# Two fp32r passes for the attention scores, gate columns on the output-gate slab, and the first block loaded ahead

## The chip, the cores and the metric

The kernel runs on one core of a Trainium2 chip. The metric is the device time of one execution in microseconds; a run is compared by the median of its timed executions, and one further execution is profiled.

## The reference

A decoder trunk of two layers over 512 tokens of width 1024, in fp32. Each layer computes, cut to what the change touches:

```python
h = rmsnorm(x, norm_mix[i])
proj = h @ w_in[i]            # 3088 columns: q 512, k 512, v 512, conv 3 x 256, gla q 128, k 128, v 256, gate 256, low-rank gate 16
q, k = rope(q), rope(k)       # 4 heads x 2 maps x 64
for each block of 128 queries: # differential attention
    s = (q @ k.T) / 8, causal
    a = softmax(s[:, map 0]) - lam * softmax(s[:, map 1])
    o_da = rmsnorm(a @ v) * gain * (1 - lam_init)
o_sc = B * conv3(C * h_in)
log_a = log_sigmoid(g_lr @ gla_w_gate2 + gla_b_gate) / 16
o_g = rmsnorm(gla(g_q, g_k, g_v, log_a)) * silu(g_r)
x = x + concat(o_da, o_sc, o_g) @ w_out[i]
x = x + peer(rmsnorm(x, norm_ffn[i]))      # 16384 single-neuron experts
```

## The kernel before

Tokens stand in four blocks of 128 (TB = 4), visited in ORDER = (3, 0, 1, 2) by the first normalisation. Each layer is `mixer` (about the first 286 us) and `peer` (the rest). Projections are done in split precision: an operand is a high part, rounded to fp32r, and a low part, the remainder, and `mm3` forms high x high, high x low and low x high in three single-pass matmuls. The split costs a ScalarE cast and a VectorE subtraction (`split`, L79).

`setup` loads all four blocks of x (L93), then the identity; `norm_T` (L176) loads the gain row, computes each block's statistics, normalises into a scratch tile and transposes it into hh and hl. Scratch is the space of va and kT.

`slab` (L234) brings a slab of w_in, 8 x 128 rows by n columns, in four quarters: a load into `wraw` (three buffers), then the split into wh and wl (two buffers each, so one slab can be prepared while another is used). `across` (L247) uses the slab as stationary operand, 24 matmuls of 512 columns per 128 slab columns; `down` (L256) uses hh and hl as stationary, 24 matmuls of n columns per token block. The slabs come in the order gla v (2560), low-rank gate (3072, 16 columns padded to 128), gla q and k (2304), output gate (2816), q and k (0 to 768, each rotated and transposed by `rope_T`), v (1024, 1280), and three for the convolution (2048, 1792, 1536).

`gla` (L483) is a generator: a first piece from the gate matmul to the cumulated decay b, then six levels that fill masked score tiles, the state recurrence, and the outputs. `fill` (L305) advances it between the slabs, against due times written by hand.

`diff_attention` (L425) multiplies, for each head and map, a query tile qz whose other map's 64 rows are zero with kT, both in fp32; then the causal mask (bf16) is added in PSUM, and VectorE and ScalarE do the softmax. Blocks 0 and 1 are computed between the convolution's slabs, blocks 2 and 3 after them, while w_out is loaded in eight rows of 128 x 1024 through two `woraw` buffers and split (L357). `out_proj` (L371) has 48 matmuls of 512 columns a token block and starts with the last normalisation's transposes.

The framework keeps each engine's instructions in an order that a planner works out at build time by priority (program order) and its own estimate of when things are ready; loads on SP's queue are in such an order too. Only instructions marked so stay in program order, in `peer`. A tile that is laid over the space of older tiles waits for their last readers.

Of the kernel before, what the change touches and what calls it, by code (L numbers as in the profile page):

```python
# [19 lines left out]
P = 128  # L20
T = 512
# [42 lines left out]
class K:  # L64
# [18 lines left out]
    def setup(self):  # L83
# [9 lines left out]
        for tb in ORDER:  # L93
            nc.sync.dma_start(self.x[:, tb], self.ins["x"][tb * P:(tb + 1) * P, :])
# [3 lines left out]
        nc.sync.dma_start(self.ident, self.ins["c_ident"])  # L98

# [101 lines left out]
    def mixer(self, L):  # L201
# [3 lines left out]
        with ExitStack() as mc:  # L205
            mp = mc.enter_context(tc.tile_pool(name="mix", bufs=1, reuse_waits="tile"))
            lamv = mp.tile([P, 4, 64], F32, name="lamv")
# [3 lines left out]
            kT = mp.tile([P, 4, T], F32, name="kT")  # L211
# [3 lines left out]
            norm = self.norm_T(ins["norm_mix"][L:L + 1, :], hh, hl, rows(va) + rows(kT), order=ORDER)  # L215
            with ExitStack() as wc:
# [7 lines left out]
                z = qp.tile([P, 2, T + 2], F32, name="z", bufs=1)  # L224
                nc.vector.memset(z[:, :, 0:2], 0.0)
# [8 lines left out]
                def slab(c0, n):  # L234
# [3 lines left out]
                    for kh in range(0, KD, 2):  # L238
                        raw = wp.tile([P, 2, w], F32, tag="wraw", name="wraw", bufs=3)
# [28 lines left out]
                wh, wl = slab(2560, 256)  # L268
                for i, tb in enumerate(ORDER):
# [11 lines left out]
                lt = mp.tile([P, 64], F32, name="lt")  # L281
# [10 lines left out]
                for j, ps in across(3072, 16):  # L292
                    nc.scalar.copy(lr, ps[0:16])
# [8 lines left out]
                side = self.gla(L, gq, gk, gv, sg, lr, mgh, mgl, gp)  # L302
# [7 lines left out]
                fill(10)  # L310
                for i in range(4):
                    for tbs, ps in down(256 * i):
                        self.rope_T(ps, (qT, kT)[i // 2], i % 2, tbs, qp)
                    fill(10 + 10.5 * (i + 1))
                for i in range(2):
                    for tbs, ps in down(1024 + 256 * i):
                        nc.scalar.copy(va[:, tbs, 256 * i:256 * i + 256], ps)
                    fill(52 + 10.5 * (i + 1))
# [4 lines left out]
                qz = [ap.tile([P, 4, 2, P], F32, name=f"qz{i}", bufs=1) for i in range(2)]  # L323
                for t in qz:
                    nc.gpsimd.memset(t, 0.0)
                heads = []

                def attend(tb):
                    heads.append(self.diff_attention(tb, qT, kT, va, qz[tb % 2], lam, ap))
# [20 lines left out]
            with tc.tile_pool(name="wout", bufs=1, reuse_waits="tile") as op_:  # L350
                wr = [op_.tile([P, D], F32, tag="woraw", name="woraw", bufs=2) for _ in range(2)]
                mh = op_.tile([P, 4, T], F32R, name="mh")
                ml = op_.tile([P, 4, T], F32R, name="ml")
# [3 lines left out]
                for k in korder:  # L357
                    raw = wr.pop(0) if wr else op_.tile([P, D], F32, tag="woraw", name="woraw", bufs=2)
# [3 lines left out]
                def chunk(k, s):  # L362
                    if k < 4:
                        return mh[:, k, s], ml[:, k, s]
                    a, b = (mch, mcl) if k < 6 else (mgh, mgl)
                    return a[:, k % 2, s], b[:, k % 2, s]
# [4 lines left out]
                def out_proj(tb):  # L371
                    for nh in range(2):
                        ps = self.psC.tile([P, T], F32, tag="c", name="pso")
                        n = slice(nh * 512, nh * 512 + 512)
                        for k in korder:
                            self.mm3(ps, *chunk(k, slice(tb * P, tb * P + P)), wh[:, k, n], wl[:, k, n],
# [5 lines left out]
                for tb in range(TB):  # L382
                    if tb > 1:
                        attend(tb)
                    t = slice(tb * P, tb * P + P)
                    self.head_out(heads[tb], dgain, mh[:, 0:4, t], ml[:, 0:4, t])
# [691 lines left out]
```

## Time and profile before

| | |
|---|---|
| median of three runs | 3034.66 us (3029.43 to 3035.7) |
| profiled execution, own time | 3031.94 us |
| its span in the profile | 3030.2 us |
| TensorE busy | 2964.8 us (98%) |
| VectorE busy | 2440.4 us (81%) |
| ScalarE busy | 1270.5 us (42%) |
| GpSimd busy | 690.1 us (23%) |
| mean DMA rate | 250 GB/s |
| mean granted TensorE clock | 0.997 |

Busy time is the union of an engine's instructions. Matmuls are pipelined, so that one that is 0.40 us long can be followed by the next after 0.23 us; what a matmul costs is read from the starts in the order of time. The span is the profiled execution from its first to its last instruction; its own time has the 1.7 us around it as well.

### The profile page before, as it was taken

Reading aid. Unit: us, or ns where it says so; the run is one execution under the profiler, and the core shown is the slowest. Engines: PE = TensorE matmul, PEld = TensorE weight load, DVE = VectorE, ACT = ScalarE, POOL = GpSimd, SP = SyncE. Lnnn points to the kernel's source line nnn. Section 1 sums busy time; section 2 is a strip of 40 time slices with the busy share of each in tenths; the row PEclk is TensorE's granted clock in tenths of the full one; section 3 lists DMA queues with packets and bytes.
Section 4 is the critical chain, followed back from the end, with each engine's and each line's share of the span. In section 5 each row is a group of like instructions: output and inputs, shape, how many; then the busy total and the mean of one; then the engine's idle time right before and its main releaser. Section 6 shows DMA issues by size and latency. Waiting matters only on the chain.

```text
span 3030.2 us, 45706 instructions
## 1 busy us (share of the span) xinstructions
PE 2964.8 (98%) x16742; PEld 2650.7 (87%) x16742; DVE 2440.4 (81%) x5057; ACT 1270.5 (42%) x1874; POOL 690.1 (23%) x553
## 2 busy tenths in 40 slices
PE   7999999999999999999999999999999999999998
PEld 7977899999999999788889788999999999988886
DVE  5766999977788787877766769999868887878777
ACT  5343346556333333333353533565563333323333
POOL 0000000222444444211100000002224544452120
PEclk9999999999999999999999999999999999999999
DMA  4212248899999998999722222579999999989996
GB/s 122 67 57 78 96 142 256 279 300 340 341 332 333 325 337 299 349 337 329 290 78 67 73 72 91 173 245 296 313 352 328 336 335 333 332 299 343 341 347 225
DMA packets 335697, 756.64 MB, mean 250 GB/s; under 512 B 31568, under 2 KB 192240, under 8 KB 331376
## 3 DMA queue, kind: packets, MB, share of 16 engines
q1 hardware_dynamic: 141936, 406.60, 37.8%
q0 software_dynamic: 73728, 268.47, 24.7%
q10 hardware_dynamic: 119808, 78.66, 8.3%
q8 instruction: 131, 2.15, 0.3%
q14 instruction: 94, 0.77, 0.1%
HBM read 672.89 MB, written 80.74 MB: 249 GB/s over the span
## 4 chain that ended last, share of the span: by engine, by line
PE 76%; DVE 11%; issue 4%; DMA 3%; ACT 3%; POOL 1%; ACTq 1%; SPq 0%; DVEq 0%; POOLq 0%
PE pv L76 10%; PE pv L77 10%; PE pv L75 10%; PE psh L75 8%; PE psh L77 8%; PE psh L76 8%; PE psp L77 2%; PE psp L76 2%; PE psp L75 2%; PE psq L75 2%; PE psq L76 2%; PE psq L77 2%; DVE ul L651 1%; DMA row<-in_v_rows,idx 1%; POOL row L737 1%
## 5 line engine op out<-in xcount | busy, mean ns | idle before, releaser
L75 PE MATMUL psh<-ahi,uh 128*128 128x384 f32 x2048 | 692.2, 338 | 6.6 <-ACT ht L665 6.6
L77 PE MATMUL psh<-ahi,ul 128*128 128x384 f32 x2048 | 687.5, 336 | 0.0
L76 PE MATMUL psh<-alo,uh 128*128 128x384 f32 x2048 | 686.3, 335 | 0.0
L737 POOL DMA_INDIRECT row<-in_u_rows,idx x256 | 364.5, 1424 | 1342.6 <-DVE si L905 689.0
L76 PE MATMUL pv<-vl,wh 128*128 128x512 f32 x1536 | 601.1, 392 | 6.9 <-DVE vl L828 6.9
L77 PE MATMUL pv<-vh,wl 128*128 128x512 f32 x1536 | 601.2, 392 | 0.0
L75 PE MATMUL pv<-vh,wh 128*128 128x512 f32 x1536 | 597.6, 390 | 0.0
L651 DVE TENSOR_TENSOR ul<-uraw,uh 128x1024 fp32r<-128x1024 f32 x288 | 350.9, 1221 | 210.8 <-ACT uh L650 200.5
L737 POOL DMA_INDIRECT row<-in_v_rows,idx x256 | 307.6, 1202 | 623.6 <-DVE yacc L754 589.9
L650 ACT CAST uh<-uraw 128x1024 fp32r<-128x1024 f32 x288 | 302.3, 1050 | 330.8 <-PE psh L76 99.5
L828 DVE TENSOR_TENSOR vl<-vraw,vh 128x1024 fp32r<-128x1024 f32 x256 | 313.1, 1223 | 128.1 <-ACT vh L833 118.3
L75 PEld LDWEIGHTS psh<-ahi,uh 128*128 128x128 f32 x2048 | 385.1, 188 | 14.1 <-ACT ht L665 9.7
L76 PEld LDWEIGHTS psh<-alo,uh 128*128 128x128 f32 x2048 | 385.1, 188 | 4.1
L77 PEld LDWEIGHTS psh<-ahi,ul 128*128 128x128 f32 x2048 | 385.0, 188 | 0.0
L76 PEld LDWEIGHTS pv<-vl,wh 128*128 128x128 f32 x1536 | 289.0, 188 | 66.8 <-DVE vl L828 8.7
L665 ACT ACTIVATE ht<-psh 128x384 f32<-128x384 f32 x256 | 125.2, 489 | 519.2 <-PE psh L77 512.6
L77 PEld LDWEIGHTS pv<-vh,wl 128*128 128x128 f32 x1536 | 289.0, 188 | 61.6 <-DVE wl L828 1.2
L754 DVE SCALAR_TENSOR_TENSOR yacc<-row,wk,yacc 128x1024 f32<-128x1024 f32 x254 | 325.1, 1280 | 18.3 <-DMA row<-in_v_rows,idx 16.8
L75 PEld LDWEIGHTS pv<-vh,wh 128*128 128x128 f32 x1536 | 289.0, 188 | 57.5
L842 ACT CAST wh<-ht 128x384 fp32r<-128x384 f32 x256 | 131.2, 512 | 492.9 <-DVE ht L840 482.0
L745 DVE SCALAR_TENSOR_TENSOR gscr<-row,xg 128x1024 f32<-128x1024 f32 x256 | 312.4, 1220 | 27.7 <-DMA row<-in_u_rows,idx 25.9
L833 ACT CAST vh<-vraw 128x1024 fp32r<-128x1024 f32 x256 | 268.5, 1049 | 7.5 <-DMA vraw<-in_v_rows 7.1
(289 smaller groups left out, 4396.3 us busy)
## 6 DMA issues: line engine op xcount, KB each, us to landing
uraw<-in_peer_u SPq DMA_DIRECT2D x256, 512.0 KB, 5.4
vraw<-in_v_rows SPq DMA_DIRECT2D x256, 512.0 KB, 6.0
G<-stg ACTq DMA_DIRECT2D x48, 1024.0 KB, 7.7
g<-G SPq DMA_DIRECT2D x32, 1536.0 KB, 10.1
H<-ht ACTq DMA_DIRECT2D x144, 192.0 KB, 4.8
ht<-H SPq DMA_DIRECT2D x144, 192.0 KB, 6.6
wraw<-in_w_in SPq DMA_DIRECT2D x96, 256.0 KB, 2.9
uraw<-in_peer_w_q SPq DMA_DIRECT2D x32, 512.0 KB, 3.5
```

The source lines that it names most:

```text
L75: mm(ps, ah, bh, start=first, stop=False)
L76: mm(ps, ah, bl, start=False, stop=False)
L77: mm(ps, al, bh, start=False, stop=last)
L650: pin(nc.scalar.copy(hi, src))
L651: self.last = pin(nc.vector.tensor_tensor(lo, src, hi.bitcast(F32), op=OP.subtract))
L665: pin(nc.scalar.activation(hs[c], ps, AF.Gelu))
L737: nc.gpsimd.indirect_dma_start(out=r, out_offset=None, in_=ins[name], in_offset=bass.IndirectOffsetOnAxis(ap=idx[:, k:k + 1], axis=0))
L745: nc.vector.scalar_tensor_tensor(sc, r, 1.0, xg, op0=OP.mult, op1=OP.mult, accum_out=hd[:, k:k + 1])
L754: nc.vector.scalar_tensor_tensor(yacc, r, wk[:, k:k + 1], yacc, op0=OP.mult, op1=OP.add)
L828: self.last = pin(nc.vector.tensor_tensor(lo, src, hi.bitcast(F32), op=OP.subtract))
L833: pin(nc.scalar.copy(vh[c], vs[c]))
L842: pin(nc.scalar.copy(wh[c], hs[c]))
```

## The change

Scores: the rotated keys are no longer stored as one fp32 tile. `rope_T` writes kd, in fp32r, for each map m: the map's 64 rows hold the high part, and the other map's 64 rows hold the low part of the same keys. A query block is written as qd, whose both halves hold the high part of map m's query, and ql with the low part. One pass qd x kd contracts 128 rows and gives high x high + high x low, a second pass of 64 rows gives low x high. The zeroed qz tiles go.

Gate columns: the 16 low-rank gate columns ride at the end of the output-gate slab, which is now 272 columns wide and comes before the gla q and k slab. Its matmuls are token-major, so the 16 columns are copied out and transposed back into lr. `gla`'s first piece is started right behind it, before the gla q and k slab; the masked query copies (qbm) move out of that piece.

Loads: only block 3 of x is loaded ahead of the identity, the gain row and the first slab; the other three follow the slab. The scratch of the first normalisation is va and qT. The slab has two wraw buffers instead of three, and the lambda vectors take one of them for a time. w_out comes in sixteen halves of 128 x 512 through three buffers; the projection of block 0 is traced before the heads of block 3, whose mh and ml are now per block (three buffers).

```diff
+        self.load_x(ORDER[0])
-        for tb in ORDER:
-            nc.sync.dma_start(self.x[:, tb], self.ins["x"][tb * P:(tb + 1) * P, :])
...
-            kT = mp.tile([P, 4, T], F32, name="kT")
+            kd = mp.tile([P, 2, 4, T], F32R, name="kd")
...
-            norm = self.norm_T(ins["norm_mix"][L:L + 1, :], hh, hl, rows(va) + rows(kT), order=ORDER)
+            norm = self.norm_T(ins["norm_mix"][L:L + 1, :], hh, hl, rows(va) + rows(qT), order=ORDER)
...
-                        raw = wp.tile([P, 2, w], F32, tag="wraw", name="wraw", bufs=3)
+                        raw = wp.tile([P, 2, w], F32, tag="wraw", name="wraw", bufs=2)
...
                 wh, wl = slab(2560, 256)
+                if L == 0:
+                    for tb in ORDER[1:]:
+                        self.load_x(tb)
...
+                lamv = wp.tile([P, 5, 64], F32, tag="wraw", name="lamv", bufs=2)
...
-                for j, ps in across(3072, 16):
-                    nc.scalar.copy(lr, ps[0:16])
+                wh, wl = slab(2816, 272)
+                for tb in range(TB):
+                    ps = self.psC.tile([P, 272], F32, tag="c", name="psg")
+                    for k in range(KD):
+                        self.mm3(ps, hh[:, k, tb * P:tb * P + P], hl[:, k, tb * P:tb * P + P], wh[:, k], wl[:, k],
+                                 k == 0, k == KD - 1)
+                    nc.scalar.copy(lt16[:, tb], ps[:, 256:272])
+                    nc.scalar.activation(sg[:, tb], ps[:, 0:256], AF.Silu)
+                trl = self.psB.tile([16, TB, P], F32, tag="b", name="trl")
+                for tb in range(TB):
+                    nc.tensor.transpose(trl[:, tb], lt16[:, tb], self.ident)
+                nc.scalar.copy(lr, trl.rearrange("p b t -> p (b t)"))
+                side = self.gla(L, gq, gk, gv, sg, lr, mgh, mgl, gp)
+                next(side)
                 for j, ps in across(2304):
...
-                for tbs, ps in down(2816):
-                    nc.scalar.activation(sg[:, tbs], ps, AF.Silu)
...
-                    nc.sync.dma_start(raw, ins["w_out"][L, k * P:(k + 1) * P, :])
-                    self.split(wh[:, k], wl[:, k], raw)
+                    for s in (slice(0, 512), slice(512, 1024)):
+                        raw = op_.tile([P, 512], F32, tag="woraw", name="woraw", bufs=3)
+                        nc.sync.dma_start(raw, ins["w_out"][L, k * P:(k + 1) * P, s])
+                        self.split(wh[:, k, s], wl[:, k, s], raw)
...
+                    if tb == TB - 1:
+                        out_proj(0)
+                    mh[tb] = op_.tile([P, 4, P], F32R, tag="mh", name="mh", bufs=3)
...
+        for m in range(2):
+            r, o = slice(64 * m, 64 * m + 64), slice(64 - 64 * m, 128 - 64 * m)
+            nc.scalar.copy(kd[r, m, hs, ts], tr[r])
+            nc.vector.tensor_tensor(kd[o, m, hs, ts], tr[r], kd[r, m, hs, ts].bitcast(F32), op=OP.subtract)
...
-        for m in range(2):
-            r = slice(64 * m, 64 * m + 64)
-            nc.scalar.copy(qz[r, :, m], qT[r, :, s])
+        for m, r in enumerate(rows):
+            for o in (r, rows[1 - m]):
+                nc.scalar.copy(qd[o, m], qT[r, :, s])
+            nc.vector.tensor_tensor(ql[r], qT[r, :, s], qd[r, m].bitcast(F32), op=OP.subtract)
...
-                nc.tensor.matmul(ps[:, 0:nk], qz[:, h, m], kT[:, h, 0:nk], start=True, stop=False)
+                nc.tensor.matmul(ps[:, 0:nk], qd[:, m, h], kd[:, m, h, 0:nk], start=True, stop=False)
+                nc.tensor.matmul(ps[:, 0:nk], ql[r, h], kd[r, m, h, 0:nk], start=False, stop=False)
```

## Rows read from the trace of the kernel before

**Rows 1.** The page's engine totals: busy us, share of the span, instructions.

```profile
PE 2964.8 (98%) x16742; PEld 2650.7 (87%) x16742; DVE 2440.4 (81%) x5057; ACT 1270.5 (42%) x1874; POOL 690.1 (23%) x553
```

**Rows 2.** Windows: length, busy by engine (instructions), granted clock, DMA share, GB/s.

```profile
0.00:13.10 13.10, 0.00 (x0) 0.00 (x0) 7.51 (x94) 7.30 (x12) 7.19 (x21) 1.00 0.82 275
...
60.00:80.00 20.00, 18.05 (x124) 16.28 (x124) 14.51 (x31) 12.94 (x20) 0.00 (x0) 0.91 0.20 53
80.00:100.00 20.00, 19.92 (x137) 16.82 (x136) 17.68 (x46) 9.18 (x17) 0.00 (x0) 1.00 0.24 67
...
209.00:240.00 31.00, 29.45 (x135) 18.74 (x133) 27.74 (x65) 19.57 (x40) 0.00 (x0) 1.00 0.40 136
240.00:286.00 46.00, 45.27 (x234) 36.45 (x233) 27.63 (x87) 14.70 (x29) 0.00 (x0) 1.00 0.14 46
```

**Rows 3.** Order of time, TensorE, single passes: start, length, operation, idle before.

```profile
31.87 0.40 PE L75 MATMUL psp<-ahi,wh 128*128 128x512 f32 x1
32.10 0.40 PE L76 MATMUL psp<-alo,wh 128*128 128x512 f32 x1
...
71.39 0.28 PE L75 MATMUL psp<-wh,ahi 128*128 128x256 f32 x1
71.51 0.28 PE L76 MATMUL psp<-wl,ahi 128*128 128x256 f32 x1
73.73 1.67 PE L552 MATMUL pst<-qs,ks 128*128 128x256 f32 x4 [1.95 <-DVE qs L544]
...
900.14 0.33 PE L76 MATMUL psh<-alo,uh 128*128 128x384 f32 x1
900.31 0.33 PE L77 MATMUL psh<-ahi,ul 128*128 128x384 f32 x1
```

**Rows 4.** Order of time, TensorE, score products and a group of transposes.

```profile
171.37 0.38 PE L438 MATMUL pss<-kT,qz 128*128 128x128 f32 x2
171.59 0.22 PE L439 MATMUL pss<-causal,identb 128*128 128x128 bf16 x1
...
209.08 1.03 PE L479 MATMUL htr<-ident,ho 128*128 128x128 f32 x8
209.95 0.81 PE L438 MATMUL pss<-kT,qz 128*128 128x384 f32 x2
...
210.65 0.86 PE L438 MATMUL pss<-kT,qz 128*128 128x384 f32 x2
211.35 0.22 PE L439 MATMUL pss<-causal,identb 128*128 128x128 bf16 x1
...
221.93 1.02 PE L438 MATMUL pss<-kT,qz 128*128 128x512 f32 x2
222.79 0.49 PE L454 MATMUL atr<-ident,e 128*128 128x128 f32 x3
```

**Rows 5.** Groups of VectorE by shape, 160 to 290: count, busy us, mean ns, idle before.

```profile
L81 DVE TENSOR_TENSOR wol<-woraw,woh 128x1024 fp32r<-128x1024 f32 x8 | 9.7, 1216 | 1.2 <-ACT woh L80 1.2
...
L81 DVE TENSOR_TENSOR wl<-wraw,wh 128x512 fp32r<-128x512 f32 x8 | 5.4, 684 | 2.4 <-ACT wh L80 2.4
```

**Rows 6.** The chain that ended last, in order of time: start, length, piece.

```profile
62.40 1.28 ACT L519
...
73.73 3.38 PE pst L552 x8
...
1580.16 1.99 PE pst L552 x8
```

**Rows 7.** Order of time, VectorE, the first normalisation.

```profile
7.54 0.16 DVE L168 SCALAR_TENSOR_TENSOR ry<-rt,ry 128x1 f32<-128x1 f32 x1
...
11.82 1.29 DVE L185 SCALAR_TENSOR_TENSOR kT<-x,ry,va 128x1024 f32<-128x1024 f32 x1
```

**Rows 8.** Instructions on wraw, 0 to 210: ns min/median/max; us to landing.

```profile
L80 ACT CAST wh<-wraw x52: 391/620/647, 11.6 to 184.7; 128x512 fp32r<-128x512 f32 x48, 128x256 fp32r<-128x256 f32 x4
...
DMA to landing us min/median/max: 1.7/2.9/8.5
```

More of the change, by code (lines that the diff above doesn't have):

```diff
@@ L322, in mixer @@
                 ap = ac.enter_context(tc.tile_pool(name="attn", bufs=2, side="right", reuse_waits="tile"))
-                qz = [ap.tile([P, 4, 2, P], F32, name=f"qz{i}", bufs=1) for i in range(2)]
-                for t in qz:
-                    nc.gpsimd.memset(t, 0.0)
+                zp = wc.enter_context(tc.tile_pool(name="conv", bufs=1, reuse_waits="tile"))
+                z = zp.tile([P, 2, T + 2], F32, name="z")
+                nc.vector.memset(z[:, :, 0:2], 0.0)
                 heads = []
                 def attend(tb):
-                    heads.append(self.diff_attention(tb, qT, kT, va, qz[tb % 2], lam, ap))
+                    heads.append(self.diff_attention(tb, qT, kd, va, lam, ap))
                 attend(0)
@@ L350, in mixer @@
             with tc.tile_pool(name="wout", bufs=1, reuse_waits="tile") as op_:
-                wr = [op_.tile([P, D], F32, tag="woraw", name="woraw", bufs=2) for _ in range(2)]
-                mh = op_.tile([P, 4, T], F32R, name="mh")
-                ml = op_.tile([P, 4, T], F32R, name="ml")
+                mh, ml = {}, {}
                 wh = op_.tile([P, KD, D], F32R, name="woh")
@@ L384, in mixer @@
                         attend(tb)
-                    t = slice(tb * P, tb * P + P)
-                    self.head_out(heads[tb], dgain, mh[:, 0:4, t], ml[:, 0:4, t])
+                    if tb == TB - 1:
+                        out_proj(0)
+                    mh[tb] = op_.tile([P, 4, P], F32R, tag="mh", name="mh", bufs=3)
+                    ml[tb] = op_.tile([P, 4, P], F32R, tag="ml", name="ml", bufs=3)
+                    self.head_out(heads[tb], dgain, mh[tb], ml[tb])
                 ac.close()
@@ L392, in mixer @@
                 for tb in range(TB):
-                    late = out_proj(tb)
+                    if tb:
+                        late = out_proj(tb)
                     if tb < TB - 1:
@@ L403, in mixer, with rope_T @@
         return xh, xl, rest()
-    def rope_T(self, ps, dst, half, tbs, pool):
+    def rope_T(self, ps, q, kd, half, tbs, pool):
         nc = self.nc
@@ L422, in rope_T, with diff_attention @@
                 nc.tensor.transpose(tr[:, h, b], t[:, b, 2 * h:2 * h + 2, :], self.ident)
-        nc.scalar.copy(dst[:, 2 * half:2 * half + 2, tbs.start * P:tbs.stop * P], tr.rearrange("p h b t -> p h (b t)"))
-    def diff_attention(self, tb, qT, kT, va, qz, lam, ap):
+        tr = tr.rearrange("p h b t -> p h (b t)")
+        hs, ts = slice(2 * half, 2 * half + 2), slice(tbs.start * P, tbs.stop * P)
+        if q is not None:
+            nc.scalar.copy(q[:, hs, ts], tr)
+            return
+        for m in range(2):
+            r, o = slice(64 * m, 64 * m + 64), slice(64 - 64 * m, 128 - 64 * m)
+            nc.scalar.copy(kd[r, m, hs, ts], tr[r])
+            nc.vector.tensor_tensor(kd[o, m, hs, ts], tr[r], kd[r, m, hs, ts].bitcast(F32), op=OP.subtract)
+    def diff_attention(self, tb, qT, kd, va, lam, ap):
         nc = self.nc
@@ L428, in diff_attention @@
         s = slice(tb * P, tb * P + P)
-        for m in range(2):
-            r = slice(64 * m, 64 * m + 64)
-            nc.scalar.copy(qz[r, :, m], qT[r, :, s])
+        qd = ap.tile([P, 2, 4, P], F32R, tag="qd", name="qd")
+        ql = ap.tile([P, 4, P], F32R, tag="ql", name="ql", bufs=1)
+        rows = [slice(0, 64), slice(64, 128)]
+        for m, r in enumerate(rows):
+            for o in (r, rows[1 - m]):
+                nc.scalar.copy(qd[o, m], qT[r, :, s])
+            nc.vector.tensor_tensor(ql[r], qT[r, :, s], qd[r, m].bitcast(F32), op=OP.subtract)
         po = self.psB.tile([P, 4, P], F32, tag="b", name="po")
@@ L437, in diff_attention @@
                 ps = self.psA.tile([P, T], F32, tag="a", name="pss")
-                nc.tensor.matmul(ps[:, 0:nk], qz[:, h, m], kT[:, h, 0:nk], start=True, stop=False)
+                r = rows[m]
+                nc.tensor.matmul(ps[:, 0:nk], qd[:, m, h], kd[:, m, h, 0:nk], start=True, stop=False)
+                nc.tensor.matmul(ps[:, 0:nk], ql[r, h], kd[r, m, h, 0:nk], start=False, stop=False)
                 nc.tensor.matmul(ps[:, tb * P:nk], self.identb, self.causal, start=False, stop=True)
@@ L506, in gla @@
             nc.gpsimd.memset(hsel[r, h:h + 1], 1.0)
-            nc.scalar.copy(qbm[r, h], gq[r])
         reset = gp.tile([P, T], F32, tag="ld", name="reset", bufs=2)
@@ L528, in gla @@
         yield 5
+        for h in range(4):
+            nc.scalar.copy(qbm[32 * h:32 * h + 32, h], gq[32 * h:32 * h + 32])
         at = gp.tile([P, TB, 4, P], F32, name="at")
```

27 lines of the change are left out of this document (13 added, 14 removed).

## The prediction

> **What bounds the kernel now.** I read the engine totals first, then windows over the mixers, then the order of time on TensorE there. The reader is to see three things. TensorE is busy for nearly the whole span and no other engine comes near it [rows 1], so a stall hidden on another engine is worth nothing, and a matmul taken off TensorE is worth its spacing wherever TensorE is the engine that is waited for. The change leaves the PEER mixer alone; it works inside the first 286 us of each layer. There TensorE has nothing for the first 13.1 us of the kernel, before data has arrived, and is then as dense as in the rest, but for waits of one or two us. Inside a mixer VectorE is second, and it is dense in two places: 17.7 of 20 us in the gated-linear-attention levels and 27.7 of 31 us where blocks 2 and 3 of the attention are computed [rows 2]. There a saving on TensorE can turn into a wait for VectorE.
>
> Busy time of a matmul overlaps the next, so I price by spacing, start to start: one fp32r pass costs 0.23 us at 512 columns, 0.173 at 384 and 0.118 at 256 [rows 3].
>
> **Scores.** Today a product of a zero-padded query and kT is an fp32 matmul that the trace shows as two instructions. The pair takes 0.22 us at 128 keys, 0.70 at 384 and 0.86 at 512 [rows 4]; between them I put 0.46 at 256. A layer has eight products (4 heads, 2 maps) of each width. The new form is two single passes: 2 x 0.118 at 256, 2 x 0.173 at 384, 2 x 0.23 at 512. Saved per product: 0.22, 0.35 and 0.40; times eight: 1.8, 2.8 and 3.2 us. No row shows an fp32r pass at 128 columns. Bounds: 0.056 (half of one of today's 0.11 us instructions, as a pass that scales with columns would cost) and 0.22 (as dear as today's whole pair). That is +0.9 to -1.8 us a layer. I take 0.11, the nearest row, so nothing saved there.
> A page of the Trainium skill speaks against the narrow case: TensorE: Matmul & The Clock Gate, section Part 2, gives loading the stationary operand a time of its columns over 1.2 GHz, 107 ns for 128, whatever the rows. By that estimate two passes with fresh weights cost 214 ns at 128 keys against 224, as good as no gain, while the sustained spacing of 81 ns that the same section states would save 0.5 us a layer; the sum moves by 1 us at most, and no run here shows which holds.
>
> How much of it arrives? For block 1 all 1.8 us, since projections stand between the products and keep TensorE full. For blocks 2 and 3 (6.0 us) VectorE is at 27.7 of 31 us, and it gets more: two subtractions of 64x512 for the low query halves per block, which cannot be cheaper than a 128x512 subtraction by partitions, 0.68 each, and sixteen half-row splits of w_out at 0.68 instead of eight at 1.22, together +1.2 us [rows 5]. If VectorE sets that stretch, nothing of the 6.0 arrives. Against that stands the next stretch: TensorE 45.3 of 46 us, VectorE only 27.6 of 46 [rows 2]. Its output-projection matmuls need only the w_out halves and finished heads; the change puts the projection of block 0 ahead of the last heads and loads w_out in three half-size buffers, so they can be pulled forward. I take two thirds, 4.0. Scores: 5.8 a layer, 11.6 together; bounds 0 (1.8 lost at 128 keys, block 1 kept, the rest held by VectorE) and 17.4.
>
> **Gate columns.** Gone: one slab of 16 columns padded to 128, 24 passes at 512 columns, 24 x 0.233 = 5.6 us [rows 3], with its four memsets, loads and splits. Added: 16 more columns on 96 passes at 0.118/256 us a column, 0.7 us, and four transposes at 0.22 (eight instructions took 0.87) [rows 4], 0.9. Net 4.0 a layer, 8.0 in all; bounds 8.0 and 9.8 (transposes free). The separate copies of 16 columns are ScalarE work, which has idle time there.
>
> **Gate chain.** TensorE waits 1.95 us for the first level's qs, after a chain of Abs, Exp, Ln (with table loads), scan and VectorE products [rows 3]; in layer 0 its next eight matmuls then take 3.38 us where layer 1's take 1.99 [rows 6], at a granted clock of 0.91 in that window [rows 2]: 1.4 us more. The change starts the chain before the q/k projection of 48 passes, 11.2 us of cover. From the first of those table loads to the level's matmuls it is 11.3 us now [rows 6], with splits between its steps, and only its last two products need q and k. Recoverable: 2 x 1.95 + 1.4 = 5.3; I take 4.5 and keep 0 to 5.3. What is late next if the cover fails is the same first level.
>
> **First block ahead.** Nothing runs on TensorE for 13.1 us while DMA moves 275 GB/s [rows 2]; the first normalisation starts at 11.82, though its statistics are done at 7.7 [rows 7]. I put that down to the gain row, which is issued behind four 512 KB blocks. With one block, the identity and the gain row ahead, 1.1 MB, the row needs 4 us of transfer at the same rate; then the statistics decide, the normalisation can start near 7.5 and the first transposes near 8.8, 4.3 us earlier. The other three blocks go behind the slab's first two quarters on SP's queue, 3.2 MB in all by then, still landing near 12. Not all of it lasts: quarters 3 and 4 of the slab now need a buffer that a split must free, and the lambda vectors take a buffer too, so the next slab can be 1 or 2 us late. Take 3.0; bounds -1 and 4.3. The rotary constants now wait until the last normalisation frees qT; they are due at the first rotation some 40 us later, so nothing.
>
> **Two slab buffers instead of three.** A quarter takes 2.9 us to land, then 0.62 on ScalarE [rows 8] and 0.68 on VectorE [rows 5]: 4.2 a turn, so two buffers bring a slab in 8.4 us, against 11.3 of matmuls that it feeds (96 x 0.118). Hidden, with 2.9 us to spare. What is queued behind a late split: the next quarter's load on SP, then TensorE. At layer 1's start three quarters can be in before they are needed and the fourth waits for a split; now the third is late as well. Charge 1.5 there and 0.5 a layer elsewhere, 2.5; bounds 0 and the rival below.
>
> **At nothing:** key rotation gains two VectorE subtractions and one half-partition copy per pair (some 5.5 us of VectorE a layer), where VectorE has 5 idle us in 20 even around the first levels [rows 2]; without that cover 5.5 a layer. Dropped memsets were on GpSimd.
>
> **Sum.** 11.6 + 8.0 + 4.5 + 3.0 - 2.5 = 24.6 us. Against the profiled execution's own 3031.94 (span 3030.2 and 1.7 around it): 3007.3. That execution is 2.7 us under the median of the three runs shown (3034.66); I place the new median half-way, 3009. Differences under 0.2%, 6.1 us, can't be told from none here.
>
> **Rivals.**
> 1. VectorE sets the attention. For it: 27.7 of 31 us plus 2.6 new. Against: the idle VectorE time right behind. Only block 1's 3.6 us of the 11.6 remain, and if the gate wait also comes back half, 24.6 - 8.0 - 2.3 = 14.3: 3018 to 3020.
> 2. All of it arrives: 17.4 + 9.8 + 5.3 + 4.3 = 36.8 without new waits: 2995 to 2998. Against: VectorE's rows.
> 3. Slower: slab starvation in the levels. In the window with VectorE at 17.7 of 20 [rows 2], a quarter's subtraction can queue behind level work; with two buffers the next load can't be issued meanwhile, and a full turn of 4.2 us minus the spare decides. Two layers have some eight slabs there; at 3.9 us each, 31 us, the kernel ends 6 us above its time: 3038 to 3042. Below 3.1 us each it still gains. Against: the 2.9 us to spare.
> 4. The changes don't move the end: the gate columns' 5.6 us were cover for the next slab's load, which then shows as a wait of like size, and scores are held as in 1: 24.6 - 8.0 - 8.0 - 3 = about 6: 3026 to 3031.
>
> **How the numbers follow.** Forecast (3002 to 3016) 0.50; rival 1 0.20; rival 2 0.12; rival 4 0.11; rival 3 0.07. The predicted time is the likeliest's. The range takes in rival 1 and part of 2 and 4: 2998 to 3027. Faster by over 0.2%: the forecast, rivals 1 and 2 and a fifth of 4, 0.84; within: the rest of 4 and a little of 3, 0.10; slower 0.06.
>
> **What would show it.** Right: two score instructions with spacing near 0.23 at 512 columns; no 16-column slab; no wait of TensorE before the first level; first matmul near 8.8 us; mixers some 12 us shorter each, and the PEER stage as long as before. Wrong: TensorE waiting for slab splits (the subtraction of the low half) in the levels or after the value projection; TensorE waiting for exponentials or the low query halves between blocks 2 and 3; pairs at 128 keys longer than 0.22.

## The result, and the profile after

The changed kernel takes 3058.85 us (median of five, 3053.81 to 3066.88) where the kernel before took 3034.66 beside it: ratio 1.0091, interval 1.0069 to 1.0113. Forecast were 3009 us and a gain. The profiled execution has a span of 3056.7 us and a mean granted clock of 0.990. The PEER stage is as long as before in layer 0 and 4.5 us longer in layer 1, and among the profiles of all runs each varies by 10 to 12 us; the loss is in the mixers. At TensorE's first query matmul of `peer` layer 0 is 11.3 us late (297.1 us instead of 285.8) and layer 1 is 22.1 us late in all.

TensorE's line of the page [rows 1] has twelve more busy microseconds, not fewer:

```profile
PE 2976.7 (97%) x16702; PEld 2653.8 (87%) x16702; DVE 2462.1 (81%) x5089; ACT 1285.0 (42%) x1918; POOL 688.5 (23%) x549
```

Windows over blocks 2 and 3 of the attention in layer 0 (busy time of each engine, then granted clock, DMA share and rate); in the kernel before the stretches here stood at full clock [rows 2]:

```profile
211.00:218.00 7.00, 5.23 (x26) 3.10 (x24) 5.40 (x11) 3.54 (x8) 0.00 (x0) 0.98 0.00 0
218.00:228.00 10.00, 10.00 (x26) 6.08 (x26) 5.98 (x16) 3.38 (x9) 0.00 (x0) 0.50 0.39 132
228.00:247.00 19.00, 18.67 (x90) 12.40 (x89) 15.92 (x39) 13.46 (x32) 0.00 (x0) 1.00 0.36 111
247.00:256.00 9.00, 5.45 (x20) 3.75 (x19) 6.91 (x23) 1.28 (x3) 0.00 (x0) 0.81 0.00 0
```

Ten whole microseconds run at 0.50, the 1.2 GHz level, with 26 matmuls (run 1 below does 48 in the same stretch). What stood ahead of it, and what happens at 247, is in the order of time on TensorE (start, duration, line, tiles; in brackets the idle time before it and who ended it):

```profile
215.22 0.48 PE L75 MATMUL pso<-woh,mgh 128*128 128x512 f32 x1
217.47 0.46 PE L467 MATMUL pss<-kd,qd 128*128 128x384 f32 x1 [1.77 <-ACT e L475]
217.86 0.68 PE L468 MATMUL pss<-kd,ql 64*128 64x384 f32 x1
...
233.62 0.22 PE L469 MATMUL pss<-causal,identb 128*128 128x128 bf16 x1
233.65 0.47 PE L467 MATMUL pss<-kd,qd 128*128 128x512 f32 x1
234.05 0.49 PE L468 MATMUL pss<-kd,ql 64*128 64x512 f32 x1
234.48 0.23 PE L469 MATMUL pss<-causal,identb 128*128 128x128 bf16 x1
...
247.55 0.48 PE L77 MATMUL pso<-woh,ml 128*128 128x512 f32 x1
251.54 0.51 PE L75 MATMUL pso<-woh,mgh 128*128 128x512 f32 x1 [3.51 <-DVE x L381]
```

and the weight loads of the same stretch, which have a row of their own:

```profile
233.62 0.19 PEld L467 LDWEIGHTS pss<-kd,qd 128*128 128x128 f32 x1
234.05 0.18 PEld L468 LDWEIGHTS pss<-kd,ql 64*128 64x128 f32 x1 [0.24 <-issue]
234.47 0.10 PEld L469 LDWEIGHTS <-identb 128*128 128x128 bf16 x1 [0.24 <-issue]
```

Three things are to be seen. The 64-row pass takes 0.43 us to the next start (234.05 to 234.48), nearly twice a 512-column pass of `mm3`: its load starts together with it at 234.05, 0.40 us behind the start of the pass ahead, and the load behind it starts late too. TensorE waits 1.77 us for exponentials, since all four PSUM tiles through which scores rotate (`psA`) are still to be read, and the half clock follows within half a microsecond. And block 1's projection waits 3.5 us for block 0's additions (L381), which VectorE does only at 250.81 and 251.55, behind the maxima and products of block 3:

```profile
250.81 0.68 DVE L381 TENSOR_TENSOR x<-x,pso 128x512 f32<-128x512 f32 x1
...
251.55 0.68 DVE L381 TENSOR_TENSOR x<-x,pso 128x512 f32<-128x512 f32 x1
```

The first level's wait, which was to go [rows 3], is longer: 61.39 to 64.29 in layer 0, as long in layer 1. ScalarE and VectorE in the order of time:

```profile
55.60 2.51 ACT L559 COPY qbm<-gq 32x512 f32<-32x512 f32 x4
58.13 1.28 ACT L571 ACT_TABLE_LOAD   x1
59.43 0.63 ACT L571 ACTIVATE ld<-ld 128x512 f32<-128x512 f32 x1
...
61.75 0.63 ACT L571 ACTIVATE ld<-ld 128x512 f32<-128x512 f32 x1 [1.06 <-DVE ld L570]
62.28 0.57 ACT L314 COPY gk<-psp 128x512 f32<-128x512 f32 x1
```

```profile
60.09 1.23 DVE L575 TENSOR_TENSOR qs<-qbm,ld 128x1024 f32<-128x1024 f32 x1 [0.85 <-ACT ld L571]
...
62.41 1.22 DVE L575 TENSOR_TENSOR qs<-qbm,ld 128x1024 f32<-128x1024 f32 x1 [0.76 <-ACT ld L571]
63.55 0.68 DVE L574 TENSOR_TENSOR ks<-gk,ld 128x512 f32<-128x512 f32 x1
```

The chain of gates did start earlier, but the query copies now stand inside it, ahead of the Exp, and the copy of gk stands behind the second level's Exp; so ks, the last operand of the first level, comes after the second level's qs. Part of the wait was there for any order: the last pass of the gla q and k projection starts at 61.39, and behind it the copy of gk (0.57 us) and ks (0.68) stand in a row, an estimate of some 1.3 us that no earlier start of the chain covers.

At the start of layer 0 the first transposes begin at 13.46 us (13.16 before) and the value projection ends 2.6 us later. VectorE there:

```profile
6.44 0.16 DVE L168 TENSOR_TENSOR rt<-ry 128x1 f32<-128x1 f32 x1
9.99 0.69 DVE L81 TENSOR_TENSOR wl<-wraw,wh 128x512 fp32r<-128x512 f32 x1 [3.40 <-ACT wh L80]
10.61 0.15 DVE L169 SCALAR_TENSOR_TENSOR rt<-rt,rv 128x1 f32<-128x1 f32 x1
...
12.12 1.29 DVE L187 SCALAR_TENSOR_TENSOR qT<-x,ry,va 128x1024 f32<-128x1024 f32 x1
```

A split of the slab (L81) stands in VectorE's order between two steps of the block's statistics and waits 3.40 us for a slab quarter that lands at 9.3 us; the statistics, whose data is there, wait behind it.

### The profile page after: what moved, and what is told of

The parts are those of the page before. It is cut to its first block, busy times and chain, and to the rows that moved or that the text cites. A ratio compares the mean times of both kernels' runs of the same rounds, so it can differ in the third digit from the quotient of the medians.

```text
span 3056.7 us, 45747 instructions
## 1 busy us (share of the span) xinstructions
PE 2976.7 (97%) x16702; PEld 2653.8 (87%) x16702; DVE 2462.1 (81%) x5089; ACT 1285.0 (42%) x1918; POOL 688.5 (23%) x549
## 3 DMA queue, kind: packets, MB, share of 16 engines
q0 software_dynamic: 73728, 268.47, 24.5%
## 4 chain that ended last, share of the span: by engine, by line
PE 75%; DVE 10%; issue 4%; DMA 4%; ACT 4%; POOL 1%; ACTq 1%; SPq 0%; POOLq 0%; DVEq 0%
PE pv L76 10%; PE pv L77 10%; PE pv L75 10%; PE psh L75 8%; PE psh L77 8%; PE psh L76 8%; PE psq L75 2%; PE psq L76 2%; PE psq L77 2%; DMA row<-in_v_rows,idx 2%; PE psp L77 2%; PE psp L76 2%; PE psp L75 2%; POOL row L768 1%; DMA uraw<-in_peer_u 1%
## 5 line engine op out<-in xcount | busy, mean ns | idle before, releaser
L859 DVE TENSOR_TENSOR vl<-vraw,vh 128x1024 fp32r<-128x1024 f32 x256 | 313.1, 1223 | 126.4 <-ACT vh L864 117.1
L75 PEld LDWEIGHTS psh<-ahi,uh 128*128 128x128 f32 x2048 | 385.6, 188 | 15.0 <-ACT ht L696 10.5
L864 ACT CAST vh<-vraw 128x1024 fp32r<-128x1024 f32 x256 | 268.5, 1049 | 11.3 <-DMA vraw<-in_v_rows 10.1
```

Of the source, the lines that this page charges most:

```text
L75: mm(ps, ah, bh, start=first, stop=False)
L859: self.last = pin(nc.vector.tensor_tensor(lo, src, hi.bitcast(F32), op=OP.subtract))
L864: pin(nc.scalar.copy(vh[c], vs[c]))
```

## The experiments

A part that is put back is as in the removed lines of the change's diff. Runs 1 to 4, 5 to 8, 9 to 12 and 13 to 15 were each made beside the same runs of the kernel before, run 16 beside its own; they stand here by subject.

**1. Old scores.** `rope_T` and `diff_attention` are as before; the rest stays changed.

```diff
-                nc.tensor.matmul(ps[:, 0:nk], qd[:, m, h], kd[:, m, h, 0:nk], start=True, stop=False)
-                nc.tensor.matmul(ps[:, 0:nk], ql[r, h], kd[r, m, h, 0:nk], start=False, stop=False)
+                nc.tensor.matmul(ps[:, 0:nk], qz[:, h, m], kT[:, h, 0:nk], start=True, stop=False)
```

> The changed kernel with the scores of the kernel before (fp32 products from the zero-padded query halves and the fp32 keys); gate columns, early gate chain, early projection, loading order and slab buffers stay as changed. Theory A (the stacked passes are dear because their weight loads stand open, and the thinner work on TensorE that this leaves is what the half-clock stretch of 10.2 us in blocks 2 and 3 follows): 32 products a layer get cheaper by 2.7 us in all, and the two stretches of 10.2 us at half clock (5 us each) go, so 3059 - 5 - 10 = 3044 us, mean granted clock near 0.995. Theory B (the early projection of block 0 and the gate chain lose the time, the scores hardly any): 3059 - 5 = 3053 us, and a stretch of some 10 us at half clock is still there in each layer.

Measured: 3034.33 us beside 3035.33, ratio 0.9999 (0.9987 to 1.001). The whole loss, 24.5 us, hangs on the scores; everything else in the change sums to nothing by the time. Theory A was too small: the 3.5 us wait goes as well, although block 0's projection is traced as in the changed kernel. The window at 218 is back at full clock:

```profile
218.00:228.00 10.00, 9.48 (x48) 6.09 (x47) 9.00 (x23) 6.98 (x17) 0.00 (x0) 1.00 0.56 179
```

**2. Second pass over all 128 rows.**

```diff
-                nc.tensor.matmul(ps[:, 0:nk], ql[r, h], kd[r, m, h, 0:nk], start=False, stop=False)
+                nc.tensor.matmul(ps[:, 0:nk], ql[:, h], kd[:, m, h, 0:nk], start=False, stop=False)
```

> The changed kernel with the second score pass over all 128 rows (both maps' low halves times the key stack) where it took one map's 64; that adds the other map's low query by low key product to each score. Theory A (a load of 64 rows waits for the 128-row pass ahead of it to finish streaming, and a load of 128 rows does not): the second pass of 512 columns goes from 0.40 to 0.23 us, of 128 from 0.25 to about 0.12, some 5 us a layer, so about 3048 us or less if the half-clock stretch shrinks too. Theory B (a change of stationary data inside one product costs this much whatever its rows): passes stay at 0.25 to 0.42 us, time 3055 to 3062 us.

Measured: 3048.69 us, ratio 1.004 (1.0027 to 1.0053): theory A. Twice the rows make the pass cheaper by 0.14 to 0.19 us, and the stretch of 10.2 us at half clock is one of 3.4 us, at 215; the wait for block 0's additions stays (4.0 us). (The other map's low by low product does not belong to the score. Low queries padded with zeros would leave it out; that was not tried.)

**3. Block 0's projection ahead of block 3's attention.**

```diff
-                    if tb > 1:
-                        attend(tb)
                     if tb == TB - 1:
                         out_proj(0)
+                    if tb > 1:
+                        attend(tb)
```

> The changed kernel with block 0's output projection traced ahead of block 3's attention, so that its two adds stand ahead of block 3's work on VectorE. Theory A (the 3.75 us wait and the 3.4 us at half clock behind it come of those adds' place in VectorE's order): 5 us a layer go, 3049 us. Theory B (VectorE has that much to do before the projections go on in any order): the wait turns up at block 3's scores or at block 1's projection, 3055 to 3062 us.

Measured: 3050.12 us, ratio 1.0038 (1.0024 to 1.0051): theory A; the wait for L381 is gone, the half clock at 217 is still there and lasts 13.7 us.

**5. Runs 2 and 3 together.**

> The changed kernel with both edits of the first runs: second score pass over all 128 rows (it adds the other map's low by low product) and block 0's projection traced ahead of block 3's attention. Theory A (two separate losses): 3059 - 10 - 9 = 3040 us. Theory B (once the passes are cheap, TensorE waits for the softmax work on VectorE and ScalarE in blocks 2 and 3 whatever the order): 3046 to 3050 us, with TensorE idle there and long stretches at half clock.

Measured: 3033.51 us, ratio 0.9992 (0.9982 to 1.0003). The two edits give 25.3 us together, more than 10.2 and 8.7 apart. TensorE still waits for exponentials, and the window at 218 follows:

```profile
214.56 0.69 PE L467 MATMUL pss<-kd,qd 128*128 128x384 f32 x1 [2.04 <-ACT e L475]
```

```profile
218.00:228.00 10.00, 9.61 (x53) 7.26 (x53) 9.35 (x24) 6.67 (x17) 0.00 (x0) 1.00 0.53 178
```

So both theories hold a part: the loss goes, but no gain is left that the times can show. Compared with run 1, whose score products cost 17.3 us a layer, these cost 12.4 (below), and the kernel is 0.8 us faster by the medians, 2 by the ratios, both inside their intervals.

**4. Gate part alone**, on the kernel before, with two slab buffers:

```diff
-                for j, ps in across(3072, 16):
-                    nc.scalar.copy(lr, ps[0:16])
...
+                wh, wl = slab(2816, 272)
+                for tb in range(TB):
...
+                side = self.gla(L, gq, gk, gv, sg, lr, mgh, mgl, gp)
+                next(side)
                 for j, ps in across(2304):
```

> The kernel before with the gate part of the change alone: gate columns on the output-gate slab, the gate chain ahead of the pass over 2304, and two buffers of raw slabs in place of three (three do not fit beside the wider slab). Scores, projections and the loading of x stay as before. Theory A (the gate part saves the slab and the products that it removes): 3035 - 8 = 3027 us or a little under, PE waiting at the first level as long as in the changed kernel (2.8 us). Theory B (the gate chain's wait and the half clock behind it in both layers eat it, or two buffers starve the slabs): 3033 to 3042 us.

Measured: 3036.72 us, ratio 0.9994 (0.9982 to 1.0006): theory B in the sum, but with two causes in it, which runs 8, 12 and 14 part.

**6. Old scores, x and three slab buffers as before.** Run 1 with

```diff
-        self.load_x(ORDER[0])
+        for tb in ORDER:
+            self.load_x(tb)
...
-                        raw = wp.tile([P, 2, w], F32, tag="wraw", name="wraw", bufs=2)
+                        raw = wp.tile([P, 2, w], F32, tag="wraw", name="wraw", bufs=3)
```

> The changed kernel with the scores of the kernel before, all of x loaded ahead as before, and three raw slab buffers as before: what is left of the change is the gate columns, the early gate chain, the early projection and the half rows of w_out. Theory A (loading one block ahead and two buffers cost the 2 us that the value projection ends later in both layers): 3034 - 4 = 3030 us. Theory B (what is late there is made up at the first level anyway): 3033 to 3035 us.

Measured: 3029.76 us beside 3035.84, ratio 0.9977 (0.9967 to 0.9987): theory A.

**7. First level traced later.**

```diff
-                fill(5)
                 for i in range(4):
                     for tbs, ps in down(256 * i):
                         self.rope_T(ps, (qT, kT)[i // 2], i % 2, tbs, qp)
+                        fill(5)
```

> As the run before it, with the first level traced behind the first half slab of the rotated queries instead of ahead of it. Theory A (the wait of 2.8 us at the first level is a matter of its place: 48 more passes, 5.7 us, cover it): the wait goes, and the half clock behind it, 2 to 4 us a layer, 3023 to 3026 us. Theory B (the levels behind it come as late as before and their chain on VectorE sets the stretch): the wait turns up at the next level, 3029 to 3031 us.

Measured: 3032.01 us, ratio 0.9988 (0.9976 to 0.9999): nothing gained, as theory B has it, but the wait turns up elsewhere, at the first rotated transposes, 2.4 us for VectorE's rotation:

```profile
PE rtr L439 <- DVE qkn L435: 2.4, 1, 2.4
```

**8. Gate chain at its old place.** Run 6 with `side = self.gla(...)` behind the projection of 2304 and without `next(side)`.

> As the run before the last, with the gate chain at its old place behind the q and k projection (old due times too), so that the gate columns and the early projection are what is left of the change. Theory A (the columns are the gain, the early chain is a loss of a wait and a half-clock stretch in each layer): 3025 to 3028 us. Theory B (the early chain has a share in the gain): slower than with it, 3032 us or more.

Measured: 3030.72 us, ratio 0.9979 (0.997 to 0.9988), between the two theories: the same as with the early chain. In the profiles layer 0's mixer is 6.9 us shorter than before, and 3.5 with the early chain: its place is worth nothing, at best.

**9. Both repairs, x ahead, old chain**, and **10. the score passes of both maps in pairs**, on top of it:

```diff
             for m in range(2):
                 ps = self.psA.tile([P, T], F32, tag="a", name="pss")
...
                 nc.tensor.matmul(ps[:, 0:nk], qd[:, m, h], kd[:, m, h, 0:nk], start=True, stop=False)
-                nc.tensor.matmul(ps[:, 0:nk], ql[:, h], kd[:, m, h, 0:nk], start=False, stop=False)
+                pss.append(ps)
+            for m in range(2):
+                nc.tensor.matmul(pss[m][:, 0:nk], ql[:, h], kd[:, m, h, 0:nk], start=False, stop=False)
+            for m, ps in enumerate(pss):
                 nc.tensor.matmul(ps[:, tb * P:nk], self.identb, self.causal, start=False, stop=True)
...
-                pss.append(ps)
```

> The stacked scores with the second pass over all rows and the early projection first (as in the fifth run), all of x loaded ahead as before, gate columns kept, gate chain at its old place. Theory A (what the old scores showed for x and the gate chain adds to the two repairs): value projection of layer 0 ends at 30.5 us instead of 32.6, 3033.5 - 4 = 3029 to 3030 us. Theory B (softmax work sets the attention and takes back what arrives early): 3033 us or more.

> As the run before, with the score passes of a head in another order: the first pass of both maps, the second pass of both, then both masks, so that no first pass but the head's first follows a mask of 29 ns. Theory A (the 0.07 to 0.09 us that the first pass costs over 0.23 and 0.118 is its weight load, open behind a matmul too short to cover it): half of them go back to 0.118 at 256 and 0.23 at 512 columns, some 1.2 us a layer of passes, 3026 to 3028 us. Theory B (it is the change of PSUM tile or of operands): the passes keep their spacing, same time as the run before.

Measured: 3029.26 us, ratio 0.9976 (0.9961 to 0.999), and 3028.82, ratio 0.9975 (0.9964 to 0.9986), beside 3036.46. Both are faster than the kernel before, by a quarter of a percent; both still have two slab buffers. The order of run 10 does to the passes what theory A says, 0.29 to 0.235 at 512 columns and 0.20 to 0.12 at 256, and nothing to the time.

**13. Run 10 with 64 rows again** in the second pass.

> As the tenth run (first passes of both maps, second passes of both, then the masks), but with the second passes over one map's 64 rows again. Theory A (a 64-row load cannot start while a pass over 128 rows streams, but may while a pass over the other 64 rows streams): the first map's second pass costs 0.40 to 0.42 us at 512 columns, the second map's 0.23, half of the loss comes back: 3028.8 + 4 = 3033 us. Theory B (any 64-row load stands open): both at 0.40, 3028.8 + 8 = 3037 us or more. Theory C (the order was what mattered): both at 0.23 to 0.30, 3029 us.

Measured: 3040.95 us beside 3033.89, ratio 1.0017 (1.0 to 1.0033), 12 us over run 10: theory B in the time, and some ten microseconds at half clock are back in each layer. A 64-row pass of 512 columns costs 0.42 to 0.43 us behind a 128-row pass. Run 13, then run 10:

```profile
236.69 0.48 PE L463 MATMUL pss<-kd,qd 128*128 128x512 f32 x1
237.10 0.49 PE L466 MATMUL pss<-kd,ql 64*128 64x512 f32 x1
237.52 0.23 PE L468 MATMUL pss<-causal,identb 128*128 128x128 bf16 x1
```

```profile
231.82 0.48 PE L463 MATMUL pss<-kd,qd 128*128 128x512 f32 x1
232.13 0.39 PE L466 MATMUL pss<-kd,ql 128*128 128x512 f32 x1
232.36 0.39 PE L76 MATMUL pso<-wol,mh 128*128 128x512 f32 x1
```

and run 10's loads, which start while the pass ahead streams (231.90 behind 231.82):

```profile
231.90 0.19 PEld L466 LDWEIGHTS pss<-kd,ql 128*128 128x128 f32 x1
232.14 0.19 PEld L76 LDWEIGHTS pso<-wol,mh 128*128 128x128 f32 x1
```

In most heads other matmuls stood between the two second passes. Where none did (12 heads of 32), theory A holds and more: the second started 3 to 4 ns after the first. Hence

**16. Run 13 with a head's two second passes kept next to each other.**

```diff
-            for m in range(2):
-                nc.tensor.matmul(pss[m][:, 0:nk], ql[rows[m], h], kd[rows[m], m, h, 0:nk], start=False, stop=False)
+            with self.tc.high_priority():
+                for m in range(2):
+                    self.tc.keep_in_program_order(
+                        nc.tensor.matmul(pss[m][:, 0:nk], ql[rows[m], h], kd[rows[m], m, h, 0:nk], start=False, stop=False))
```

> As the thirteenth run (64 rows, passes of both maps), with the two second passes of a head, which read the two halves of the rows, kept next to each other on TensorE, where other matmuls stood between most of them. In 12 of 32 heads of the thirteenth run they happened to be neighbours, and started 3 to 4 ns apart. Theory A (two 64-row loads of different halves, and their passes, run side by side, so that a pair costs what one did): a pair takes 0.26 to 0.43 us instead of up to 0.85, about 0.22 a pass at 512 columns, and the long half-clock stretch goes: 3029 to 3033 us. Theory B (the open load ahead of the pair and the one behind it still set off the loss): the pair is cheaper, but the half clock of 10 us a layer stays: 3036 to 3041 us.

Measured: 3032.81 us beside 3035.8, ratio 0.9991 (0.9978 to 1.0004): theory A. 30 of 32 pairs are neighbours now, and a pair of 512 columns takes 0.42 us (235.90 to 236.32; the two share a line, x2):

```profile
235.57 0.40 PE L463 MATMUL pss<-kd,qd 128*128 128x512 f32 x1
235.90 0.50 PE L468 MATMUL pss<-kd,ql 64*128 64x512 f32 x2
236.32 0.51 PE L75 MATMUL pso<-woh,mh 128*128 128x512 f32 x1
```

and the window at 218 is at full clock, behind a stretch of 3.4 us at half clock from 214.2:

```profile
218.00:228.00 10.00, 10.00 (x53) 6.97 (x52) 9.61 (x24) 6.86 (x17) 0.00 (x0) 1.00 0.50 158
```

Of the stacked forms without the loss, this one alone adds no product that does not belong to the score.

**11. First block alone** and **12. two slab buffers alone**, each on the kernel before.

> The kernel before with the loading of x alone changed: first block, identity, gain row, then the first slab's loads, then the other blocks. Theory A (prediction's step): first matmul at about 9 us instead of 13.2, end 3032 us. Theory B (the transfers share the same DMA rate, so the slab or the later blocks are late in exchange, as the value projection in the changed kernel): first matmul at 13 us, value projection at most 2 us later than before, 3035 to 3037 us.

> The kernel before with two raw slab buffers instead of three, nothing else. Prediction's step: 2.5 us in all, 1.5 of it at layer 1's start: 3037 us. Rival: the ring of two is never waited for, 3035 us; or a starved slab in the levels costs 3.9 us each, over 3041 us.

Measured: 3037.28 us, ratio 1.0006 (0.9993 to 1.0019), and 3043.73, ratio 1.0022 (1.001 to 1.0034), beside 3036.46. In run 11 the first transposes start at 13.87 us and layer 0's mixer ends 3.2 us later, which the times can hardly show. In run 12 the first level of layer 1 waits a microsecond longer than before (1.9 there), and a slab cast shows as a wait:

```profile
PE pst L552 <- DVE qs L544: 2.9, 1, 2.9
PE psp L75 <- ACT wh L80: 0.6, 1, 0.6
```

Two stretches of 3.4 us at half clock, from 1534.7 and from 1592.7, which layer 1 does not have before, cost another 3.4 us there.

**14. Gate columns alone** (with w_out in half rows): run 8 without the early projection.

> As the eighth run (old scores, x and three slab buffers as before, gate chain at its old place), with block 0's projection at its old place too: the gate columns, and w_out in half rows, alone. The prediction's term is 8.0: 3028 us. Rival: the early projection has a share of the eighth run's gain of 6: 3030 to 3033 us.

Measured: 3029.81 us, ratio 0.9981 (0.9969 to 0.9994): the early projection has no share in run 8's gain that the times can show. The half rows of w_out were not run without the columns, but the columns' part stands ahead of them: from the first transposes to the first level it is 56.2 us in layer 0 and 57.1 in layer 1, where it was 60.6 and 61.6 before, 4.4 less in each.

**15. Gain row ahead of the other blocks.** Run 8 with

```diff
                 next(norm)
+                if L == 0:
+                    for tb in ORDER[1:]:
+                        self.load_x(tb)
                 wh, wl = slab(2560, 256)
```

and only the first block loaded in `setup`.

> As the eighth run, with the loads in the order first block of x, identity, gain row, other blocks, slab. Theory A (the prediction's reason, the gain row behind four blocks, was right, and the slab's splits between the steps of the statistics were what spoiled it): the first normalisation starts before 9 us and the first transposes at 9 to 10 us; the value projection then waits for the slab, which lands at 11.6 us, so that it ends 1 us earlier at most: 3029 to 3031 us. Theory B (something else holds the normalisation): it starts at 11.8 us as before.

Measured: 3030.57 us, ratio 0.9989 (0.9975 to 1.0002). Theory A: the normalisation starts at 8.86 us and the transposes at 10.20, but then TensorE stands for the slab, which now lands last, and the value projection ends 2.1 us later than before:

```profile
8.86 1.29 DVE L187 SCALAR_TENSOR_TENSOR qT<-x,ry,va 128x1024 f32<-128x1024 f32 x1 [1.31 <-DMA va<-in_norm_mix]
```

```profile
10.20 1.97 PE L191 MATMUL psn<-ident,qT 128*128 128x128 f32 x8 [10.20 <-DVE qT L187]
15.36 0.58 PE L75 MATMUL psv<-wh,ahi 128*128 128x256 f32 x1 [3.19 <-ACT wh L80]
```

## Why the prediction was wrong

**Scores: the step that failed.** "The new form is two single passes: 2 x 0.118 at 256, 2 x 0.173 at 384, 2 x 0.23 at 512." Those spacings are of chains of full 128-row passes [rows 3], whose loads run under the pass ahead. Medians from one start to the next, 16 of each width in both layers' attention, in us:

| form | 128 keys | 256 | 384 | 512 | x8, a layer |
|---|---|---|---|---|---|
| old pair (run 1) | 0.22 | 0.43 | 0.65 | 0.86 | 17.3 |
| changed: first + second pass | 0.24 + 0.26 | 0.25 + 0.31 | 0.72 at full clock | 0.32 + 0.42 | 20.2 |
| second pass of 128 rows (run 5) | 0.14 + 0.12 | 0.20 + 0.12 | 0.26 + 0.18 | 0.29 + 0.24 | 12.4 |
| pairs of passes (run 10) | 0.15 + 0.12 | 0.12 + 0.12 | 0.26 + 0.18 | 0.24 + 0.24 | 11.4 |

The products became 2.9 us a layer dearer where 7.8 were to be saved (5.8 of them to arrive), and at 128 keys the pair is 0.49, over even the dearer bound, 0.22 a pass and so 0.44. The old pairs were also put a little too dear, 0.46 and 0.70 at 256 and 384 keys where the medians are 0.43 and 0.65, 0.6 us a layer. The rest of the 24.5 us is what follows: in layer 0, 10 us at half clock (5 lost), 3.5 us of wait for block 0's additions and 3.4 us at half clock behind it (1.7), and 0.6 us more wait for exponentials. With the 2.9 that makes some 14 us, and the mixer lost 12.0 against run 1. The prediction's sum had no term for half clock that the change brings. Key rotation, put at nothing, is not where the time went: up to the first score product the changed kernel's mixers are 0.2 and 1.0 us longer than run 1's. That the long stretch comes with lone 64-row passes is shown (runs 1, 2, 5, 13 and 16); the wait ahead of it alone does not make it, since run 5 waits 2.04 us at the same place and has 3.4 us of half clock.

**How much arrives.** Prediction: two thirds. Repaired, the products save 4.9 us a layer against run 1, and of these 0.9 and 1.3 us arrive in the two layers, from the first score product to `peer`'s first query matmul. That stretch lies behind the loads of x and the gate part (two slab buffers alone add 0.3 and 0.9 us to it, run 12). It is 113.8 to 115.0 us with the old scores (runs 1 and 8), 113.7 to 114.9 with the repaired ones (runs 5, 9 and 10), and 126.3 and 126.4 in the changed kernel. Against run 1, run 5 waits 2.7 us a layer for exponentials instead of 1.1 and has a stretch of 3.4 us at half clock (1.7 lost), which run 1 has not; that is most of what does not arrive. The direction is rival 1's, and stricter than it was put: in run 5's window at 218 VectorE is busy for 9.35 of 10 us, ahead of it TensorE waits for exponentials, and run 10's cheaper passes bring nothing more. No run took work off VectorE, so that VectorE sets the stretch is argued and not shown. The 2.6 us of new work that rival 1 gave it counts the query subtractions of one block; with both blocks' it is 3.9.

**Gate columns.** Predicted 8.0; runs 8 and 14 measure 5.1 and 4.1 by the medians, 6 by the ratios, and the profiles have 5.7 to 6.9 in layer 0's mixer and 3.3 to 3.6 in layer 1's. Mechanism right, size about right: 4.4 us a layer at the first level where 4.0 was predicted, 9 to 10.5 us in the mixers, of which the times show half or so; rival 4 is out.

**Gate chain.** Predicted -4.5, measured nothing (runs 6 and 8). The wait was put down to the start of the chain; the rows show what is late next: the query copies inside it and the copy of gk. That "only its last two products need q and k" was true, but ks is one of them and needs the last pass of that projection, so the projection is no cover for it. Even past that the rotations wait (run 7). In the changed kernel the half clock follows the wait in both layers, at 64 and 1580 us, where only layer 0 had it before.

**First block ahead.** Predicted -3.0, bounds -1 and 4.3 of gain; the profile of run 11 has 3.2 us of loss. The gain row was the reason for the late normalisation (run 15), but two steps failed: the splits of the slab entered VectorE's order between the steps of the statistics, and the same data has to come in before the value projection can go on, so whatever is put last is late.

**Two slab buffers.** Predicted 2.5, measured 7.3 by the medians (ratio 3.0 to 10.3 us): in the mixers 1.1 us in layer 0 and 5.5 in layer 1. That is the direction of rival 3, but not its price: TensorE's waits for slab casts are 1.3 us in layer 0 and 0.6 in layer 1, not 3.9 for each slab, and 3.4 of the 5.5 are half clock. The 1.5 us charged at layer 1's start did not come; that wait is 1.5 us before and in run 12.

Sum as measured: +24.5 for the scores; for the columns, the gate chain, the loads of x and the slab buffers -4 to -6, 0, +1 to +3 and +3 to +10, which run 1, having all of them and the early projection, puts at -1 together, inside its noise of some 4 us. That is the 24 us of the result.

The prediction left open which price a narrow pass has; with full rows the two passes at 128 keys take 0.26 us (run 5). The Trainium skill, TensorE: Matmul & The Clock Gate, Part 2, says that a load's time depends on its columns and not on its rows. As a duration the traces agree nearly (183 ns for 64 rows, 192 for 128, run 2 and the changed kernel), though not with the 107 ns that the prediction took from there, and the duration is not what the pass costs. Part 3 of that page of the Trainium skill lists that loads overlap matmuls in flight only where the row groups differ (the paragraph on the mechanism ahead of the list also lets a load go ahead into a background weight buffer), and says that such tiles start some 4 ns apart. The pairs of run 16 agree with the latter, 3 to 4 ns. With the list the traces do not agree: 128-row loads run under 128-row passes (run 10), and the loads that stand open are those of 64 rows behind 128.

## What to carry to other kernels

Price a new matmul by rows of the same shape and with the same neighbours: here a 64-row pass among 128-row passes costs about twice the full one, so pad it to 128 rows where the extra products are harmless, or put two that use different halves next to each other. A saving on TensorE between softmax steps arrives only as far as VectorE and ScalarE let it, and when TensorE runs dry there, a wait of two microseconds can cost five more at half clock. Of a bundle of edits measure each alone: here one good edit, the gate columns, pays for three that lose or bring nothing, and once the passes are mended the stacked scores bring hardly more than the old ones (runs 1, 5 and 8 to 10).

## What was not expected of the hardware

- A 64-row fp32r weight load does not run under a 128-row pass ahead of it: 0.42 us a 512-column pass where a 128-row pass takes 0.23 (runs 10 and 13, 12 us of the kernel with the half clock that comes with it). Two of different halves side by side take 0.42 together (run 16).
- A pass behind the 29 to 39 ns mask matmul shows its own load: 0.29 at 512 and 0.20 at 256 columns, 0.235 and 0.12 when another score pass stands ahead (runs 5 and 10).
- Stretches at the 1.2 GHz level of some 10 us a layer came with lone 64-row passes (changed kernel, runs 3 and 13), and not with the old pairs (run 1), the full-row passes behind a wait as long (runs 2 and 5) or the neighbours (run 16); there it is 3.4 us or none. What in the passes decides it stays open.
